# A two-layer decoder trunk on one core: five modulation units from TensorE to wide VectorE units, unit ends spread over later steps, running sums seeded and read by ScalarE

## The chip, the core and the metric

The kernel runs on one NeuronCore of a Trainium2 chip. The metric is the device time of one launch in microseconds (us). Five engines work from their own in-order queues: TensorE (PE; its weight loads are listed apart as PEld), VectorE (DVE), ScalarE (ACT), GpSimd (POOL, hardly used here) and SyncE (SP, which issues nearly all transfers).

## The reference

A trunk of two decoder layers over 256 tokens of width 2048, all in fp32. In both layers a mixer and an MLP are wrapped in RMSNorm and in a modulation by a condition vector `c`:

```python
cond = jax.nn.silu(c)
for i in range(DEPTH):
    mod = cond @ ada_w[i] + ada_b[i]
    sh1, sc1, g1, sh2, sc2, g2 = [m[:, None, :] for m in jnp.split(mod, 6, axis=-1)]
    h = rms_norm(x, norm_mix_g[i]) * (1.0 + sc1) + sh1
    y = even_mixer(h, ...) if i % 2 == 0 else odd_mixer(h, ...)
    x = x + g1 * y
    h = rms_norm(x, norm_mlp_g[i]) * (1.0 + sc2) + sh2
    x = x + g2 * (jnp.square(jax.nn.relu(h @ mlp_up[i])) @ mlp_down[i])
return rms_norm(x, final_norm_g)
```

`ada_w[i]` is 2048 x 12288: each of the six sections (shift, scale, gate; twice) is a product of one vector with a 2048 x 2048 matrix. The even mixer has 16 heads of attention between an input and an output projection, the odd mixer has 8 heads with a forget gate and 8 heads with three branches. `mlp_up` is 2048 x 8192, `mlp_down` 8192 x 2048.

## The kernel before

**Weights.** Every weight comes from HBM once, in pieces of 1 MB, into one of four staging buffers (`wst`); the modulation weights (`wa`) share these buffers with the projections' (`w`). Each fp32 weight is split in two: ScalarE writes the rounded high part `wh` (L306), VectorE the rest `wl` (L308), in halves of 128x1024, two to a piece, with four buffers each. A product is then three TensorE matmuls: high by high, high by low, low by high. A staging buffer is free again when `wl` of its second half is written.

**Passes.** The even input projection and the first half of layer 0's up-projection are streamed by row groups of the contraction: `kproj` (L361) takes one 1 MB piece (one of half that size in the first two groups), 48 matmuls (24), and adds into running sums that lie in SBUF between the groups. Each pass has two sums of 128x512. From the second group on, the second sum is seeded: ScalarE copies it back to PSUM before the matmuls (L370) and out again after them (L390). The first sum starts from zero in PSUM, and VectorE adds it to the stored one afterwards (L392). There are 56 such passes: 4 x 8 in the even projection (`even`, L603), 3 x 8 in the up-projection (`up_streamed`, L659). PSUM holds four `mm` tiles, two passes' worth. Other projections (`proj`, `down`) hold their sums in PSUM through.

**Modulation units.** `ada` (L226) is a generator; one unit computes some columns of one or two sections, in steps of 1 MB. On VectorE a unit accumulates `acc += w * cond[k]` (L245, L248), one operation for each of the 16 k-tiles; on TensorE it makes 16 row products into one `row` bank, four to a step (L241), and ScalarE copies the row to `acc` (L254). The unit's end turns the row into columns: four TensorE transposes for each 512 columns into the single bank `aux` (L258), a reduction on VectorE that empties it (L260), and small operations that write `mod` (L265, L268). The end stands directly behind the last step; a unit of 1024 columns has two such blocks, and the second needs the bank that the first one's reduction empties.

**The order of the work.** `queue` lists the units; `pump` runs one step of the first; `tick` is called after each weight load and pumps by a rate set for each stage; `need(left, keys)` pumps until no more than `left` units of a section are left. So the steps are woven between the loads, and SP issues weights and modulation weights in that order. A scheduler may then move an instruction past its neighbours on its engine, which shows in the order below. The norm of a row group's input (`make_h`) needs its shift and scale, and stands behind a `need`.

**Attention.** `causal_head` (L574) serves 16 even heads and 8 odd ones; VectorE scales both parts of the probabilities (L586, L590).

## Time and profile before

| | |
|---|---|
| Median of 3 runs | 2322.27 us (2320.33 to 2328.7) |
| The profiled execution | 2327.63 us, span of its instructions 2325.8 us |
| TensorE busy | 2243.2 us (96%) |
| TensorE weight loads busy | 2156.4 us (93%) |
| VectorE busy | 1669.5 us (72%) |
| ScalarE busy | 1114.7 us (48%) |
| Moved by the transfers | 599.94 MB, mean 258 GB/s |

The stages in the profile: the even input projection to some 215 us, its last row group with the even attention to some 312 us, the even output projection to some 410 us, the streamed up-projection to some 610 us, the rest of layer 0's MLP to 1180 us, the odd mixer to some 1605 us, and the second MLP to the end. A matmul's end in the profile is modelled and matmuls are pipelined, so a stretch in which TensorE is 96% busy can hold fewer matmuls than it might; the count of records of a stretch and the granted clock tell more. Every fp32 matmul of a row product leaves two records.

### The profile page before, as it was taken

Reading aid. Unit: us, or ns where it says so; the run is one execution under the profiler, and the core shown is the slowest. Engines: PE = TensorE matmul, PEld = TensorE weight load, DVE = VectorE, ACT = ScalarE, POOL = GpSimd, SP = SyncE. Lnnn points to the kernel's source line nnn. Section 1 sums busy time; section 2 is a strip of 40 time slices with the busy share of each in tenths; the row PEclk is TensorE's granted clock in tenths of the full one; section 3 lists DMA queues with packets and bytes.
Section 4 is the critical chain, followed back from the end, with each engine's and each line's share of the span. In section 5 each row is a group of like instructions: output and inputs, shape, how many; then the busy total and the mean of one; then the engine's idle time right before and its main releaser. Section 6 shows DMA issues by size and latency. Waiting matters only on the chain.

```text
span 2325.8 us, 44699 instructions
## 1 busy us (share of the span) xinstructions
PE 2243.2 (96%) x18762; PEld 2156.4 (93%) x18762; DVE 1669.5 (72%) x2456; ACT 1114.7 (48%) x1742; POOL 4.6 (0%) x25
## 2 busy tenths in 40 slices
PE   7899999999999999999999999998999999999998
PEld 5799789899999999999999988998999999999998
DVE  3888888797767777787876988888644654655555
ACT  4555753555744344344444555444544543543543
POOL 0000000000000000000000000000000000000000
PEclk9999999999999999999999999999999999999999
DMA  9899688899978778787857877886655656656652
GB/s 308 322 326 357 228 281 319 278 323 316 321 280 290 271 272 305 274 313 267 311 198 244 310 266 245 329 302 230 197 199 188 194 199 190 192 199 192 191 194 95
DMA packets 285819, 599.94 MB, mean 258 GB/s; under 512 B 14290, under 2 KB 23346, under 8 KB 285618
## 3 DMA queue, kind: packets, MB, share of 16 engines
q1 hardware_dynamic: 285072, 596.34, 74.2%
q8 instruction: 147, 2.41, 0.4%
q10 hardware_dynamic: 546, 0.75, 0.1%
q14 instruction: 54, 0.44, 0.1%
HBM read 594.95 MB, written 2.10 MB: 257 GB/s over the span
## 4 chain that ended last, share of the span: by engine, by line
issue 65%; PE 21%; DVE 7%; DMA 5%; ACT 2%; SPq 0%; POOL 0%; POOLq 0%; DVEq 0%; ACTq 0%
PE mm L386 6%; PE mm L320 6%; DMA wa<-in_ada_w_dram 3%; DVE wl L308 3%; DVE acc L248 2%; PE bank L386 1%; PE row L241 1%; PE mm L329 1%; PE mm L330 1%; PE mm L328 1%; DMA w<-in_odd_w_out_dram 1%; PE bank L593 1%; PE bank L556 1%; ACT wh L306 1%; DVE sacc L155 0%
## 5 line engine op out<-in xcount | busy, mean ns | idle before, releaser
L308 DVE TENSOR_TENSOR wl<-w,wh 128x1024 fp32r<-128x1024 f32 x736 | 878.9, 1220 | 415.2 <-ACT wh L306 414.3
L306 ACT ACTIVATE wh<-w 128x1024 fp32r<-128x1024 f32 x736 | 751.6, 1055 | 855.4 <-PE mm L320 673.4
L320 PE MATMUL mm<-hs,wh 128*128 128x256 f32 x5120 | 886.2, 278 | 3.9 <-DVE hs L408 3.0
L320 PEld LDWEIGHTS mm<-hs,wh 128*128 128x128 f32 x5120 | 776.6, 189 | 5.5 <-DVE hs L408 3.2
L320 PE MATMUL mm<-xs,wh 128*128 128x256 f32 (+1 forms) x4128 | 720.4, 279 | 2.4 <-ACT xs L454 2.2
L320 PE MATMUL mm<-hs,wl 128*128 128x256 f32 x2560 | 711.4, 278 | 4.0 <-DVE wl L308 3.8
L320 PEld LDWEIGHTS mm<-xs,wh 128*128 128x128 f32 (+1 forms) x4128 | 627.8, 189 | 5.6 <-ACT xs L454 3.4
L320 PE MATMUL mm<-xs,wl 128*128 128x256 f32 x2064 | 572.8, 279 | 1.7 <-DVE wl L308 1.6
L320 PEld LDWEIGHTS mm<-hs,wl 128*128 128x128 f32 x2560 | 482.8, 189 | 6.3 <-DVE wl L308 6.0
L248 DVE SCALAR_TENSOR_TENSOR acc<-wa,cond,acc 128x1024 f32<-128x1024 f32 (+1 forms) x360 | 389.1, 1081 | 108.3 <-DMA wa<-in_ada_w_dram 104.0
L320 PEld LDWEIGHTS mm<-xs,wl 128*128 128x128 f32 x2064 | 388.2, 188 | 3.3 <-DVE wl L308 2.8
L386 PE MATMUL mm<-xs,wh 128*128 128x256 f32 x1792 | 318.4, 281 | 0.3 <-ACT wh L306 0.3
L386 PEld LDWEIGHTS mm<-xs,wh 128*128 128x128 f32 x1792 | 273.9, 189 | 19.2 <-issue 9.2
L386 PE MATMUL mm<-xs,wl 128*128 128x256 f32 x896 | 249.6, 279 | 3.1 <-DVE wl L308 3.1
L386 PEld LDWEIGHTS mm<-xs,wl 128*128 128x128 f32 x896 | 169.2, 189 | 4.8 <-DVE wl L308 3.7
L390 ACT ACTIVATE u<-mm 128x512 f32<-128x512 f32 x88 | 51.7, 589 | 70.3 <-PE mm L386 69.5
L565 ACT ACTIVATE p<-p,st 128x128 f32<-128x128 f32 (+1 forms) x96 | 40.2, 420 | 29.3 <-DVE st L579 14.7
L536 ACT ACTIVATE t<-mm 128x256 f32<-128x256 f32 x96 | 36.4, 379 | 34.1 <-PE mm L320 24.6
L386 PE MATMUL mm<-wh,xs 128*128 128x256 f32 x256 | 50.0, 290 | 0.9 <-ACT wh L306 0.8
L258 PE MATMUL aux<-cst,acc 128*128 128x128 f32 x192 | 31.5, 285 | 19.6 <-DVE s L260 10.2
L241 PE MATMUL row<-wa,cond 128*32 128x512 f32 x288 | 47.1, 628 | 2.1 <-DMA wa<-in_ada_w_dram 2.1
L151 ACT ACTIVATE t<-xT 128x256 f32<-128x256 f32 x60 | 24.6, 414 | 45.3 <-DVE xT L471 45.3
(214 smaller groups left out, 1458.2 us busy)
## 6 DMA issues: line engine op xcount, KB each, us to landing
wa<-in_ada_w_dram SPq DMA_DIRECT2D x160, 1024.0 KB, 6.2
w<-in_mlp_up_dram SPq DMA_DIRECT2D x128, 1024.0 KB, 5.7
w<-in_mlp_down_dram SPq DMA_DIRECT2D x128, 1024.0 KB, 5.1
w<-in_odd_w_in_dram SPq DMA_DIRECT2D x44, 1024.0 KB, 5.7
wa<-in_ada_w_dram SPq DMA_DIRECT2D x64, 512.0 KB, 5.9
w<-in_even_w_in_dram SPq DMA_DIRECT2D x27, 1024.0 KB, 7.0
w<-in_even_w_out_dram SPq DMA_DIRECT2D x16, 1024.0 KB, 5.3
w<-in_odd_w_out_dram SPq DMA_DIRECT2D x16, 1024.0 KB, 6.5
```

The costliest lines, as they stand in the source:

```text
L151: A.activation(s, xT[:, kt, :], AF.Square)
L241: T.matmul(row[32 * i:32 * i + 32, :], cond[:, k:k + 1].to_broadcast([128, 32]), w[:, i, :], start=t == 0, stop=t == KT // kn - 1, tile_po ...
L248: V.scalar_tensor_tensor(acc, w[:, i, :], cond[:, k:k + 1], acc, op0=ALU.mult, op1=ALU.add)
L258: T.transpose(ps[:, i, :], acc[:, 512 * b + 128 * i:512 * b + 128 * i + 128], ident)
L306: A.activation(wh, w[:, g:g + KS, :], AF.Copy)
L308: V.tensor_tensor(wl, w[:, g:g + KS, :], wh.bitcast(F32), op=ALU.subtract)
L320: T.matmul(P[0:m, 0:S], st[:, c0:c0 + m], mv, start=f and i == 0, stop=e and i == 2)
L328: T.matmul(Ps[j][:, 0:n], hi, wh[:, c0:c0 + n], start=f, stop=False)
L386: T.matmul(Ps[i][:, 256 * h:256 * h + 256], st, mv, start=first and e == 0, stop=last and e == 2, skip_group_check=True)
L390: A.activation(flat[i], P, AF.Copy)
L536: A.activation(r, P[:, 0:S], AF.Relu)
L565: A.activation(p[:, o:o + n], p[:, o:o + n], AF.Exp, bias=m[:, i:i + 1], accum_out=den[:, i:i + 1])
```

## The change

Five things change.

1. Which units run where. The first gate (section 2) had four TensorE units of 512 columns, and now has two, and one VectorE unit of 1024. The second scale and shift (4 and 3) had eight units of 512 columns, two of them on TensorE, and are now four VectorE units that hold 512 columns of both. The second gate (5) had four units, one on TensorE, and now has two VectorE units of 1024. Five TensorE units go; the number of 1 MB steps stays.
2. The ends. `columns` puts each block of a unit's end on a list; `tick` takes one block from it before it pumps, and `need` empties it.
3. `down` of the even output projection calls `need` for the first gate inside its blocks instead of all of it ahead.
4. `kproj` seeds both sums on ScalarE and reads both out on ScalarE.
5. `NORM_A`: ScalarE scales the 256 wide part of the probabilities.

```diff
-G1_T = "1111"
-SC2_T = "0000"
-SH2_T = "0101"
-G2_T = "0100"
-NORM_A = False
+NORM_A = True
...
                 if t == KT // kn - 1:
...
+                    columns(l, secs, c0, cw, tensor, acc)
                 yield t == KT // kn - 1
+        late = deque()
+
+        def columns(l, secs, c0, cw, tensor, acc):
+            red = s32()
+            blocks = cw * len(secs) // 512
+
+            def block(b):
+                ps = aux((128, 4, 128))
+                for i in range(4):
+                    T.transpose(ps[:, i, :], acc[:, 512 * b + 128 * i:512 * b + 128 * i + 128], ident)
+                src = ps.rearrange("p a (j q) -> p a j q", q=32)[:, :, :, 0] if tensor else ps
+                V.tensor_reduce(red[:, 4 * b:4 * b + 4], src, AX.X, ALU.add)
+                if b < blocks - 1:
+                    return
...
+            for b in range(blocks):
+                late.append(lambda b=b: block(b))
...
         def tick():
+            if late:
+                late.popleft()()
             credit[0] += rate[0]
...
             while sum(k in keys for k, _ in fill) > left:
                 pump()
+            while late:
+                late.popleft()()
...
-            seeded = [g > 0 and not held and i == 1 for i in range(len(outs))]
+            seeded = g > 0 and not held
...
-                        if g == 0 or held or seeded[i]:
-                            A.activation(flat[i], P, AF.Copy)
-                        else:
-                            V.tensor_tensor(flat[i], P, flat[i], op=ALU.add)
+                        A.activation(flat[i], P, AF.Copy)
...
-        def down(W, row0, tiles, order, ev):
+        def down(W, row0, tiles, order, ev, lazy=None):
...
+                    if lazy and n == 3:
+                        need(max(2 - blk, 0), lazy)
...
-                need(3 - g, (l, 3))
+                need(3 - g, (l, 4))
...
+        queue(0, (2,), True, 0, 512)
+        queue(0, (2,), True, 512, 512)
+        queue(0, (2,), False, 1024, 1024)
         for g in range(4):
-            queue(0, (2,), G1_T[g] == "1", 512 * g, 512)
-        for g in range(4):
-            queue(0, (4,), SC2_T[g] == "1", 512 * g, 512)
-            queue(0, (3,), SH2_T[g] == "1", 512 * g, 512)
-        for g in range(4):
-            queue(0, (5,), G2_T[g] == "1", 512 * g, 512)
+            queue(0, (4, 3), False, 512 * g, 512)
+        for c0 in (0, 1024):
+            queue(0, (5,), False, c0, 1024)
...
-        need(0, (0, 2))
-        down(even_w_out[0], 0, o, (2, 3, 0, 1), residual(0, 2, True))
+        down(even_w_out[0], 0, o, (2, 3, 0, 1), residual(0, 2, True), (0, 2))
```

ScalarE in the streamed up-projection, before; the numbers tell buffers apart, `mm` are the passes' sums in PSUM, `u` the stored ones:

```order
L390 ACTIVATE u_4587<-mm_5286 128x512
L370 ACTIVATE mm_5425<-u_4591 128x512
L306 ACTIVATE wh_5479<-w_5477 128x1024
L306 ACTIVATE wh_5483<-w_5477 128x1024
L390 ACTIVATE u_4589<-mm_5356 128x512
L370 ACTIVATE mm_5494<-u_4593 128x512
L306 ACTIVATE wh_5548<-w_5546 128x1024
```

The same place now (L401 is the eviction, L382 the seeding, L318 the split):

```order
L318 ACTIVATE wh_5444<-w_5442 128x1024
L401 ACTIVATE u_4574<-mm_5319 128x512
L382 ACTIVATE mm_5457<-u_4578 128x512
L401 ACTIVATE u_4575<-mm_5320 128x512
L318 ACTIVATE wh_5448<-w_5442 128x1024
L382 ACTIVATE mm_5458<-u_4579 128x512
L318 ACTIVATE wh_5513<-w_5511 128x1024
```

Before, both splits of `w_5477`, whose pass writes `mm_5494`, stood behind the eviction of the pass three before (`mm_5286`). Now the second split of `w_5442`, whose pass writes `mm_5457` and `mm_5458`, stands behind both evictions of the pass two before (`mm_5319`, `mm_5320`).

VectorE in layer 0's MLP, at the end of a layer 1 unit, before; `s` is the reduced end, `aux` the transposes' bank:

```order
L308 TENSOR_TENSOR wl_9516<-w_9509,wh_9515 128x1024
L245 TENSOR_SCALAR acc_9686<-wa_9687,cond_100 128x1024
L260 TENSOR_REDUCE s_9523<-aux_9524 128x4
L308 TENSOR_TENSOR wl_9589<-w_9586,wh_9588 128x1024
L260 TENSOR_REDUCE s_9523<-aux_9530 128x4
L308 TENSOR_TENSOR wl_9593<-w_9586,wh_9592 128x1024
L265 TENSOR_TENSOR mod_99<-s_9523,adab_98 128x8
```

The same unit's end now (L264 is the reduction, L244 the accumulation, L320 the low half):

```order
L320 TENSOR_TENSOR wl_9736<-w_9733,wh_9735 128x1024
L264 TENSOR_REDUCE s_9620<-aux_9679 128x4
L320 TENSOR_TENSOR wl_9740<-w_9733,wh_9739 128x1024
L244 SCALAR_TENSOR_TENSOR acc_9751<-wa_9814,cond_100,acc_9751 128x1024 x2
L320 TENSOR_TENSOR wl_9807<-w_9804,wh_9806 128x1024
L264 TENSOR_REDUCE s_9620<-aux_9743 128x4
L320 TENSOR_TENSOR wl_9811<-w_9804,wh_9810 128x1024
L271 TENSOR_TENSOR mod_99<-s_9620,adab_98 128x8
```

The two reductions stood one low half apart, the first behind the next unit's first operation; they now stand a whole load apart.

TensorE at the third row group of the up-projection, before; the unit whose end `aux_6215` is runs out inside a pass:

```order
L386 MATMUL mm_6223<-xs_96,wl_6199 128x256
L258 MATMUL aux_6215<-cst_94,acc_6213 128x128 x4
L386 MATMUL mm_6223<-xs_96,wh_6198 128x256 x2
L386 MATMUL mm_6223<-xs_96,wl_6199 128x256
L386 MATMUL mm_6222<-xs_96,wh_6198 128x256 x2
L386 MATMUL mm_6222<-xs_96,wl_6199 128x256
```

And now, where `mm_5666` is the last pass of one row group and `mm_5766` the first of the next:

```order
L398 MATMUL mm_5666<-xs_96,wl_5656 128x256
L262 MATMUL aux_5719<-cst_94,acc_5088 128x128 x4
L262 MATMUL aux_5725<-cst_94,acc_5088 128x128 x4
L398 MATMUL mm_5766<-xs_96,wh_5752 128x256
L398 MATMUL mm_5767<-xs_96,wh_5752 128x256
L398 MATMUL mm_5835<-xs_96,wh_5822 128x256
L398 MATMUL mm_5766<-xs_96,wh_5752 128x256
```

The transposes stood inside a pass; at this group and at the next both blocks now stand between two groups' passes.

## Rows read from the trace of the kernel before

**Rows 1.** Five stretches: length, busy us (x records) by engine, granted clock, transfer share, GB/s.

```profile
60.00:215.00 155.00, 139.76 (x1136) 135.84 (x1134) 138.33 (x156) 79.81 (x111) 0.00 (x0) 0.96 0.93 330
215.00:312.00 97.00, 96.54 (x704) 75.19 (x704) 74.29 (x198) 68.81 (x155) 0.00 (x0) 1.00 0.69 248
405.00:640.00 235.00, 225.20 (x1896) 210.56 (x1895) 183.82 (x257) 141.40 (x214) 0.69 (x1) 0.98 0.90 309
640.00:1180.00 540.00, 520.70 (x4473) 515.73 (x4472) 409.58 (x483) 222.84 (x291) 0.00 (x0) 0.98 0.81 287
1605.00:2326.00 721.00, 707.97 (x6186) 704.95 (x6186) 400.08 (x519) 326.25 (x462) 1.31 (x2) 0.99 0.57 183
```

**Rows 2.** TensorE's waits, 640 to 1605 us: who for whom, us in total, times, longest.

```profile
PE aux L258 <- DVE s L260: 9.4, 6, 4.2
PE mm L320 <- DVE wl L308: 5.4, 11, 1.0
...
PE aux L258 <- DVE acc L248: 2.0, 1, 2.0
```

**Rows 3.** TensorE's waits, 405 to 640 us, the longest in total.

```profile
PE aux L258 <- DVE acc L248: 6.1, 3, 3.9
```

**Rows 4.** Timeline of VectorE at 843 us: start, us, operation, [idle before it, ended by].

```profile
843.37 0.75 DVE L245 TENSOR_SCALAR acc<-wa,cond 128x1024 f32<-128x1024 f32 x1 [4.10 <-DMA wa<-in_ada_w_dram]
844.03 0.68 DVE L260 TENSOR_REDUCE s<-aux 128x4 f32<-128x512 f32 x1
844.63 1.21 DVE L308 TENSOR_TENSOR wl<-w,wh 128x1024 fp32r<-128x1024 f32 x1
```

**Rows 5.** Four stretches of 10 us around unit ends, columns as in rows 1.

```profile
495.00:505.00 10.00, 7.79 (x54) 7.79 (x55) 9.67 (x16) 5.94 (x10) 0.00 (x0) 0.83 0.92 322
764.00:774.00 10.00, 8.17 (x58) 7.97 (x57) 6.72 (x10) 2.01 (x2) 0.00 (x0) 0.83 0.61 213
840.00:850.00 10.00, 5.76 (x31) 5.56 (x30) 5.66 (x8) 0.30 (x1) 0.00 (x0) 0.66 0.56 194
...
1588.00:1598.00 10.00, 8.48 (x61) 8.22 (x62) 5.33 (x8) 3.73 (x4) 0.00 (x0) 0.83 0.99 368
```

**Rows 6.** Timeline of TensorE at 528 us, one step of a unit.

```profile
528.07 1.06 PE L241 MATMUL row<-wa,cond 128*32 128x512 f32 x8
529.06 0.50 PE L386 MATMUL mm<-xs,wh 128*128 128x256 f32 x2
```

**Rows 7.** The row products' line, in 215 to 312 and in 405 to 640 us.

```profile
L241 PE MATMUL row<-wa,cond x120: 592/592/617, 220.6 to 311.2; 128*32 128x512 f32 x120
...
L241 PE MATMUL row<-wa,cond x96: 592/616/1062, 407.4 to 610.7; 128*32 128x512 f32 x96
```

**Rows 8.** Groups by line and shape: busy us, mean ns | idle before, ended by.

```profile
L306 ACT ACTIVATE wh<-w 128x1024 fp32r<-128x1024 f32 x736 | 751.6, 1055 | 855.4 <-PE mm L320 673.4 <-PE mm L330 34.2 <-PE mm L386 33.9
L248 DVE SCALAR_TENSOR_TENSOR acc<-wa,cond,acc 128x1024 f32<-128x1024 f32 x225 | 288.1, 1280 | 89.5 <-DMA wa<-in_ada_w_dram 87.3
L248 DVE SCALAR_TENSOR_TENSOR acc<-wa,cond,acc 128x512 f32<-128x512 f32 x135 | 101.0, 748 | 18.8 <-DMA wa<-in_ada_w_dram 16.7
L390 ACT ACTIVATE u<-mm 128x512 f32<-128x512 f32 x88 | 51.7, 589 | 70.3 <-PE mm L386 69.5
L392 DVE TENSOR_TENSOR u<-mm,u 128x512 f32<-128x512 f32 x56 | 38.3, 685 | 8.0 <-PE mm L386 7.9
L370 ACT ACTIVATE mm<-u 128x512 f32<-128x512 f32 x56 | 33.3, 595 | 5.8 <-DVE u L392 5.6
L151 ACT ACTIVATE t<-xT 128x256 f32<-128x256 f32 x60 | 24.6, 414 | 45.3 <-DVE xT L471 45.3
L590 DVE TENSOR_SCALAR p<-p,st 128x256 f32<-128x256 f32 x24 | 8.3, 347 | 0.0
```

**Rows 9.** The chain of waits at 329 us: start, us, what.

```profile
329.44 5.48 PE mm L320 x48
```

**Rows 10.** TensorE's waits, 60 to 215 us, the longest in total.

```profile
PE bank L386 <- ACT xs L454: 6.9, 3, 3.3
```

More of the change, by code (lines that the diff above doesn't have):

```diff
@@ L249, in ada @@
                 if t == KT // kn - 1:
-                    n = cols // 128
-                    red = s32()
                     if tensor:
@@ L254, in ada @@
                         A.activation(acc, row, AF.Copy)
-                    for b in range(n // 4):
-                        ps = aux((128, 4, 128))
-                        for i in range(4):
-                            T.transpose(ps[:, i, :], acc[:, 512 * b + 128 * i:512 * b + 128 * i + 128], ident)
-                        src = ps.rearrange("p a (j q) -> p a j q", q=32)[:, :, :, 0] if tensor else ps
-                        V.tensor_reduce(red[:, 4 * b:4 * b + 4], src, AX.X, ALU.add)
-                    k0, n = c0 // 128, cw // 128
-                    for z, s in enumerate(secs):
-                        m = mod[:, 6 * l + s, k0:k0 + n]
-                        a0 = 96 * l + 16 * s + k0
-                        V.tensor_tensor(m, red[:, n * z:n * z + n], adab[:, a0:a0 + n], op=ALU.add)
-                        if s in (1, 4):
-                            g0 = (0 if s == 1 else 32) + 16 * l + k0
-                            V.scalar_tensor_tensor(m, m, 1.0, colA[:, g0:g0 + n], op0=ALU.add, op1=ALU.mult)
-                yield t == KT // kn - 1
+                    columns(l, secs, c0, cw, tensor, acc)
+                yield t == KT // kn - 1
+        late = deque()
[10 more added lines that the diff above has]
+                    return
+                k0, n = c0 // 128, cw // 128
+                for z, s in enumerate(secs):
+                    m = mod[:, 6 * l + s, k0:k0 + n]
+                    a0 = 96 * l + 16 * s + k0
+                    V.tensor_tensor(m, red[:, n * z:n * z + n], adab[:, a0:a0 + n], op=ALU.add)
+                    if s in (1, 4):
+                        g0 = (0 if s == 1 else 32) + 16 * l + k0
+                        V.scalar_tensor_tensor(m, m, 1.0, colA[:, g0:g0 + n], op0=ALU.add, op1=ALU.mult)
+            for b in range(blocks):
+                late.append(lambda b=b: block(b))
         fill = deque()
@@ L365, in kproj @@
             Ps = held or [mm_tile() for _ in outs]
-            seeded = [g > 0 and not held and i == 1 for i in range(len(outs))]
+            seeded = g > 0 and not held
             flat = [dst.rearrange("p a b -> p (a b)") for _, _, dst in outs]
-            for i, P in enumerate(Ps):
-                if seeded[i]:
+            if seeded:
+                for i, P in enumerate(Ps):
                     A.activation(P, flat[i], AF.Copy)
@@ L382, in kproj @@
                             tri3 = ((hi, wh[:, c:c + n]), (hi, wl[:, c:c + n]), (lo, wh[:, c:c + n]))
-                        first = h == 0 and k == 0 and not seeded[i] and not (held and g)
+                        first = h == 0 and k == 0 and not seeded and not (held and g)
                         last = h == 1 and k == kn - 1 and (end or not held)
```

## Prediction

> **What bounds the kernel now.** I read the summed busy times first, then the stretches, then who waits for whom. TensorE is busy nearly everywhere, but [rows 1] show four regimes. From 1605 us on, TensorE is busy 708 of 721 us and nothing that the change touches can shorten it. In 60 to 215 us VectorE is busy 138 of 155 us and the transfer engines 0.93: three resources are near their limits together. In 215 to 312 us, the even layer's attention, TensorE is busy 96.5 of 97 us, VectorE 74.3 and ScalarE 68.8. In 405 to 640 us, the streamed up-projection, the transfer share is 0.90 and TensorE misses 9.8 us. In 640 to 1180 us it misses 19.3 us, at a mean clock of 0.98.
>
> Much of what TensorE misses is one wait. At the end of a unit four transposes stand in TensorE's queue, and everything behind them waits until VectorE has the unit's sum, or has emptied the one bank that the transposes write. After 640 us these waits are 9.4 and 2.0 us [rows 2], in the up-projection 6.1 us [rows 3]. The worst is seen in [rows 4]: VectorE sits 4.10 us for the transfer of the next unit's weights, the reduction that empties the bank stands behind that, and TensorE's second four transposes behind the reduction. What follows costs again: [rows 5] give the mean granted clock of the 10 us around four such waits as 0.83, 0.83, 0.66 and 0.83. The clock has two levels, 1.2 and 2.4 GHz, so a mean of 0.83 over 10 us loses 1.7 us and 0.66 loses 3.4 us.
>
> **The change part by part.**
>
> *Five units leave TensorE.* A unit is 16 row products in four steps. One step on TensorE runs from 528.07 to 529.06, 0.99 us, and the plain matmuls go on directly behind it [rows 6]. Twenty steps go. Eight records make a step, so the attention stretch holds 120/8 = 15 and the up-projection 96/8 = 12 [rows 7]; all 12 go, and the other 8 go from the first gate's four units, two of which leave TensorE, in the attention. That is 7.9 us in the attention and 11.9 us in the up-projection, 19.8 us in sum, if TensorE sets the pace there (zero if it does not).
>
> *Wide units on VectorE.* 112 operations of 128x1024 at 1.28 us replace 144 of 128x512 at 0.748 us [rows 8]: 143 against 108 us, so VectorE gets 35 us for the five units and the joining of the others. All of it must lie beside TensorE's work.
>
> *Sums by ScalarE.* VectorE loses 56 adds of 0.685 us, 38.4 us, and 24 scalings of 0.347 us, 8.3 us; net of the wide units it has 11 us less. ScalarE gets 56 x (0.595 + 0.589) = 66.3 us, and 24 scalings for which no row stands; the nearest is a plain 128x256 activation of 0.414 us [rows 8], 9.9 us. Less five row copies, each about as long as a seeding, ScalarE gets 73 us on some 1115 of 2326. Cover: 48 matmuls of this shape, one pass, stand in the chain of waits with 5.48 us [rows 9], of which the last one's tail is hidden, so some 5.4 us; ScalarE now needs in that time two splits of 1.055 us, two seedings and two evictions [rows 8], 4.5 us. It fits, with 0.9 us to spare. In the order the second split of a pass now stands behind the evictions of the pass two before, where earlier both stood behind the one three before: the lead falls from about three passes to two. If that cover fails everywhere, the whole 66 us show.
>
> *The attention.* ScalarE there gets 8 x 1.18 us for the last row group's passes and 0.41 us for each of about 12 heads, less two row copies, some 13 us on 68.8, in a stretch that would shrink to 89: 0.92 busy. VectorE loses 9.7 us and gets six or so wide steps of 2.56 us: 0.9 busy. Of the 7.9 us I take half, 4 us; bounds -4 (both engines as tight as the 0.89 of VectorE in 60 to 215 us, where TensorE missed 10%, would eat the gain and more) and 7.9.
>
> *The up-projection.* For: 11.9 us of steps, 6.1 us of waits, 1.7 us of low clock. Against: the order shows that the last step of three units now falls just before a row group's first matmuls, at two of these with both blocks of transposes in front of them. The price of one such place has a row: TensorE waits up to 3.3 us for the first operand of a group in 60 to 215 us [rows 10]. There the blocks are woven into the pass before; here the second reduction, 0.68 us as the one at 844.03 in [rows 4], and its transposes come on top, so 3.3 to 4.5 us; two places at 4 us, and 1.7 us of low clock behind each, cost 11.4 us. Left are 8.3 us. A stretch 8 us shorter needs a transfer share of 0.93, which 60 to 215 us reached, but the second split's later place holds each staging buffer longer; I take 6 us, bounds -6 (all gain lost, both places at 4.5 us with two low stretches) and 14.
>
> *60 to 215 us.* 24 adds, 16.5 us, leave VectorE, which was 0.89 busy, but transfers were at 0.93 and two group ends now come later by up to 1.5 us each because their blocks are no longer woven into the last pass. I take 0, bounds -6 and +6 (a transfer share of 0.97). The Trainium skill (DMA: Bandwidth & Descriptors, Measured) states 425 GB/s for large transfers on a single core. The rows show 330 GB/s at 0.93 of the engines' time, which scales to 355, and the busiest stretch of [rows 5] has 368 at 0.99. By the page's figure transfers would bind neither here nor in the up-projection, and the sum would gain some 8 us more; by the rows it does not.
>
> *Ends spread over later steps, after 640 us.* Each block's transposes now come at the next load, one pass of 5.4 us later, and the two blocks of a unit one pass apart. The longest wait was 4.2 us [rows 2], under one pass, so this cover holds. The 11.4 us of waits and 1.7 + 3.4 + 1.7 = 6.8 us of low clock [rows 5] make 18.2 us. What comes late next is the low half of the next weights: in [rows 4] it is written at 844.63, when TensorE would have had about one pass left from 840. That covers it barely, so I take 16 us; bounds 5 and 18.2.
>
> *The rest.* The need before the output projection now falls inside it, and three forced steps in a row go with it; they are among the 15. The scalings of the odd layer move where TensorE is busy 98%: nothing.
>
> Sum: 4 + 6 + 0 + 16 = 26 us. The profiled execution took 2327.63 us (span 2325.8), 5.4 over the median of 2322.27 us; I take the 26 us from the median: **2296 us**.
>
> **The rivals.**
>
> *More: everything adds.* The attention gives 7.9, the up-projection 14, 60 to 215 us gives 6, the ends 18.2, and the early dips as much again as two of [rows 5], 5: 51 us, 2271 us. For it speaks that VectorE is relieved where it was tightest; against it ScalarE's 0.92 in the attention.
>
> *Only the ends pay.* Transfers pace the first 640 us and the TensorE steps were covered: 16 us, 2306 us. For it speaks the 0.90 to 0.93.
>
> *The waits change places.* VectorE still waits in order for the next unit's transfer, so TensorE waits for the low halves instead of the transposes; there are already 5.4 us of that after 640 us [rows 2]. The ends then give 5 us and the rest 5: 2312 us, no change that can be told.
>
> *ScalarE paces the seeded passes (slower).* Place: the 56 seeded passes up to 610 us. A late transfer holds the first split, behind it stand the evictions, behind them the seedings that TensorE needs for its next pass. The Trainium skill (TensorE: Matmul & The Clock Gate, Part 1) states that ScalarE's queue is strictly first in, first out. That is the rule by which this rival happens; the trace agrees as far as ScalarE stood idle 69.5 us before evictions until TensorE was done [rows 8], with splits queued behind them. Price: 66 us times the share that TensorE sees. It decides from 26/66 = 40% on; at 60% the time is 2322 - 26 + 40 = 2336 us. Against it: 4.5 us of work in a 5.4 us pass.
>
> That the change does not do what it says is excluded by the order: 20 steps, 56 adds and 24 scalings are gone from their engines.
>
> **How the numbers follow.** A measurement of this kernel tells about 0.5%, 11.6 us, from no change. Chances: forecast (2282 to 2309 us) 0.55, more 0.14, only the ends 0.10, waits change places 0.13, ScalarE paces 0.08. Faster by over 0.5% is the first three, 0.79, less 0.02 for the upper tail of "only the ends": 0.77; within 0.5% 0.15; slower 0.08. The range keeps "more" and "waits change places" and leaves out the last rival and half of the tails: 2266 to 2318 us.
>
> **What would show it.** Right: no wait of TensorE at transposes over 1 us after 640 us; mean clock 1.0 where [rows 5] show less; two waits of 3 to 5 us for the operands of the third and fourth group of the up-projection; the attention 3 to 5 us shorter with ScalarE near 0.9. Wrong: TensorE waiting for seedings or splits of ScalarE in most passes before 610 us, or as many microseconds for low halves after 640 us as it now has for transposes.

## The result, and the profile after

The changed kernel takes 2338.66 us (median of 5 runs, 2335.19 to 2342.5), the kernel before in the same comparison 2325.86 us: a ratio of 1.006, 95% interval 1.0041 to 1.008. It is slower by 13 us; 26 us less had been forecast, and the range ended at 2318. The profiled execution's span is 2337.7 us, 11.9 over that of before.

The same stretches as in [rows 1], of the changed kernel (length, busy us and records of TensorE, its weight loads, VectorE, ScalarE and GpSimd, granted clock, transfer share, GB/s):

```profile
60.00:215.00 155.00, 139.50 (x1122) 135.07 (x1124) 123.76 (x124) 104.36 (x158) 0.00 (x0) 0.94 0.93 327
215.00:312.00 97.00, 87.58 (x606) 70.79 (x606) 75.61 (x186) 81.36 (x182) 0.00 (x0) 0.96 0.65 231
...
405.00:640.00 235.00, 206.93 (x1723) 203.87 (x1722) 186.23 (x214) 157.62 (x246) 1.67 (x1) 0.93 0.88 298
640.00:1180.00 540.00, 522.66 (x4530) 516.64 (x4529) 413.57 (x474) 228.60 (x300) 0.00 (x0) 1.00 0.82 291
```

TensorE has less work and does not get done sooner. In 405 to 640 us it was busy 225.2 of 235 us and is now busy 206.9, at a clock of 0.93 instead of 0.98; in the attention 96.5 of 97 us, and now 87.6. In 640 to 1180 us it is busy 2 us more. What it waits for, 405 to 640 us (who for whom, us in total, times, longest), beside [rows 3]:

```profile
PE mm L398 <- ACT xs L463: 10.7, 4, 3.1
PE aux L262 <- DVE s L264: 9.4, 2, 5.2
```

And 640 to 1180 us, beside [rows 2]:

```profile
PE mm L332 <- DVE wl L320: 13.6, 24, 1.7
```

The long waits at transposes after 640 us are gone, as forecast. The waits for low halves (5.4 us in [rows 2]) are 13.6 us.

Cut into three by the weight matmuls in the traces, one profiled execution each: from the start to the first matmul of the streamed up-projection, from there to its last, and from that to the first matmul of the second MLP (us; the ratio is to the kernel before on the same chip). Everything behind that point takes 718 us in both kernels.

| kernel | up to the up-projection | up-projection | on to the second MLP | ratio (95%) |
|---|---|---|---|---|
| before | 417.3 | 199.9 | 990.9 | 1 |
| changed | 423.8 | 204.8 | 991.3 | 1.006 (1.0041 to 1.008) |
| ends_woven | 427.2 | 188.3 | 989.1 | 0.9973 (0.9959 to 0.9986) |
| sums_by_vector | 428.6 | 209.1 | 984.6 | 1.0052 (1.0035 to 1.0069) |
| scaling_by_vector | 419.7 | 206.0 | 985.5 | 1.0029 (1.0014 to 1.0044) |
| only_deferred | 423.1 | 194.1 | 990.9 | 1.001 (0.9995 to 1.0025) |
| only_wide | 426.0 | 190.0 | 989.2 | 0.9994 (0.9972 to 1.0015) |
| woven_scaling_v | 423.8 | 184.3 | 985.0 | 0.993 (0.9903 to 0.9956) |
| woven_inline | 416.4 | 192.1 | 981.4 | 0.9928 (0.9909 to 0.9948) |
| woven_sums_v | 426.0 | 188.0 | 977.9 | 0.9929 (0.9912 to 0.9945) |
| delayed_steps | 422.2 | 185.7 | 987.3 | 0.9945 (0.9923 to 0.9967) |
| deferred_delayed | 422.8 | 195.5 | 992.4 | 1.0026 (1.0006 to 1.0047) |
| steps_behind_low | 424.3 | 184.4 | 959.7 | 0.9812 (0.9791 to 0.9832) |
| deferred_behind_low | 424.6 | 194.6 | 955.0 | 0.9871 (0.9849 to 0.9893) |
| before_behind_low | 420.3 | 198.5 | 963.3 | 0.989 (0.9866 to 0.9914) |
| after_behind_low | 422.8 | 210.9 | 960.3 | 0.9932 (0.9912 to 0.9952) |

The 11.8 us are 6.5 before the up-projection, 4.9 in it and 0.4 behind it. Each third needs its own explanation. How far such a figure can be trusted is seen in the last four kernels: up to the end of the up-projection they have the same program as woven_scaling_v, only_deferred, the kernel before and the changed kernel, and differ from these by 0.5 to 3.0 us ahead of the up-projection and by 0.1 to 6.1 us in it. A difference of a few microseconds between two rows is therefore a hint and no proof; the ratios come from several executions each.

### The profile page after: what moved, and what is told of

Read it like the earlier page. It is cut to its first block, busy times and chain, and to the rows that moved or that the text cites. A ratio compares the mean times of both kernels' runs of the same rounds, so it can differ in the third digit from the quotient of the medians.

```text
span 2337.7 us, 44422 instructions
## 1 busy us (share of the span) xinstructions
PE 2228.4 (95%) x18602; PEld 2155.9 (92%) x18602; DVE 1665.0 (71%) x2341; ACT 1180.1 (50%) x1873; POOL 5.6 (0%) x25
## 4 chain that ended last, share of the span: by engine, by line
PE 38%; issue 34%; DMA 12%; DVE 11%; ACT 4%; SPq 0%; POOL 0%; DVEq 0%; POOLq 0%; ACTq 0%
PE mm L332 22%; DMA wa<-in_ada_w_dram 10%; PE mm L398 8%; DVE wl L320 5%; DVE acc L244 3%; ACT wh L318 1%; PE bank L398 1%; PE mm L342 1%; PE mm L341 1%; PE mm L340 1%; PE bank L604 1%; DMA w<-in_even_w_in_dram 1%; DVE s L264 1%; PE row L237 1%; ACT u L401 1%
## 5 line engine op out<-in xcount | busy, mean ns | idle before, releaser
L320 DVE TENSOR_TENSOR wl<-w,wh 128x1024 fp32r<-128x1024 f32 x736 | 880.2, 1220 | 412.8 <-ACT wh L318 405.7
L318 ACT ACTIVATE wh<-w 128x1024 fp32r<-128x1024 f32 x736 | 752.7, 1055 | 821.9 <-PE mm L332 670.6
L332 PE MATMUL mm<-hs,wl 128*128 128x256 f32 x2560 | 709.7, 277 | 11.4 <-DVE wl L320 11.1
L244 DVE SCALAR_TENSOR_TENSOR acc<-wa,cond,acc 128x1024 f32<-128x1024 f32 x330 | 422.7, 1281 | 140.0 <-DMA wa<-in_ada_w_dram 136.0
L401 ACT ACTIVATE u<-mm 128x512 f32<-128x512 f32 x144 | 83.9, 590 | 58.1 <-PE mm L398 57.2
L382 ACT ACTIVATE mm<-u 128x512 f32<-128x512 f32 x112 | 65.4, 598 | 1.2
```

Source lines behind the costliest of these rows:

```text
L244: V.scalar_tensor_tensor(acc, w[:, i, :], cond[:, k:k + 1], acc, op0=ALU.mult, op1=ALU.add)
L318: A.activation(wh, w[:, g:g + KS, :], AF.Copy)
L320: V.tensor_tensor(wl, w[:, g:g + KS, :], wh.bitcast(F32), op=ALU.subtract)
L332: T.matmul(P[0:m, 0:S], st[:, c0:c0 + m], mv, start=f and i == 0, stop=e and i == 2)
L382: A.activation(P, flat[i], AF.Copy)
L401: A.activation(flat[i], P, AF.Copy)
```

## Experiments on the up-projection

**Where TensorE stands there.** The timeline of the changed kernel at the third row group's start, TensorE, then VectorE, then ScalarE (start, us, operation, [idle before it, ended by]):

```profile
518.86 0.60 PE L262 MATMUL aux<-cst,acc 128*128 128x128 f32 x4
524.63 1.12 PE L262 MATMUL aux<-cst,acc 128*128 128x128 f32 x4 [5.17 <-DVE s L264]
528.87 1.23 PE L398 MATMUL mm<-xs,wh 128*128 128x256 f32 x4 [3.12 <-ACT xs L463]
```

```profile
521.27 1.23 DVE L320 TENSOR_TENSOR wl<-w,wh 128x1024 fp32r<-128x1024 f32 x1 [2.57 <-ACT wh L318]
522.69 1.28 DVE L244 SCALAR_TENSOR_TENSOR acc<-wa,cond,acc 128x1024 f32<-128x1024 f32 x1 [0.20 <-DMA wa<-in_ada_w_dram]
523.89 0.68 DVE L264 TENSOR_REDUCE s<-aux 128x4 f32<-128x512 f32 x1
...
527.79 1.28 DVE L462 SCALAR_TENSOR_TENSOR t<-xT,mod,sacc 128x256 f32<-128x256 f32 x3
```

```profile
520.18 1.06 ACT L318 ACTIVATE wh<-w 128x1024 fp32r<-128x1024 f32 x1 [3.33 <-DMA w<-in_mlp_up_dram]
```

Read from the bottom: a weight transfer lands late, so ScalarE idles 3.33 us and splits at 520.18; VectorE's low half waits for that split, behind it stand a unit step and then the reduction that empties the transposes' bank; TensorE's second four transposes wait 5.17 us for the reduction. Behind them the second reduction and the scale must be done before the group's operands exist: another 3.12 us. The group that starts at 583.25 waits 4.20 and 3.09 us in the same way, the one at 472.90 2.98 us. The stretches around the two worst have a granted clock of 0.68 and 0.66:

```profile
518.00:530.00 12.00, 3.71 (x22) 3.07 (x22) 9.22 (x16) 5.40 (x9) 0.00 (x0) 0.68 0.94 334
573.00:585.00 12.00, 4.71 (x29) 4.07 (x28) 10.97 (x19) 6.31 (x11) 0.00 (x0) 0.66 0.96 337
```

**ends_woven** changes one number of the changed kernel, so that the same units end earlier in the order:

```diff
-R_OUT = 0.7
+R_OUT = 0.9
```

> The changed kernel with one number altered: the rate of modulation steps in the output projection is 0.9 instead of 0.7, so that two more steps are done there and every unit of the up-projection ends one to three passes ahead of its row group instead of at the group's first matmul. Theory A (unit ends that stand at the group boundaries cost the time): the three boundary waits that the trace of the changed kernel shows in the up-projection, 3.7, 8.7 and 7.7 us, fall to 3 us or less each and 3 to 4 us of low clock go with them: 12 to 16 us less than the changed kernel's 2338.7, so 2323 to 2327 us. Theory B (transfers pace the first 640 us and TensorE only waits elsewhere): 2336 to 2339 us, with the waits reappearing as waits for splits. Theory C (ScalarE's seedings pace the passes): 2335 to 2339 us.

Measured: 0.9973 where the changed kernel has 1.006, 0.9 per cent or some 20 us less, at least what theory A asked for. The up-projection takes 188.3 us instead of 204.8. Two steps moved ahead of it with the new number, but that explains little: it moves 60.2 MB there, the changed kernel 61.4. Its stretch and TensorE's longest wait from 405 to 640 us:

```profile
405.00:640.00 235.00, 220.46 (x1886) 217.51 (x1886) 196.91 (x221) 166.22 (x262) 1.60 (x1) 0.98 0.93 322
```

```profile
PE mm L398 <- ACT mm L382: 5.6, 8, 1.7
```

No wait at transposes is left among the longest, the clock is back at 0.98, and the transfers, which theory B took for the limit, move 322 GB/s where they moved 298. A wait for ScalarE's seedings appears, 5.6 us in eight pieces: theory C's mechanism exists, at a twelfth of its full price of 66 us.

**sums_by_vector** and **woven_sums_v** put the running sums back as they were, in the changed kernel and in woven_scaling_v (next section):

```diff
-            seeded = g > 0 and not held
+            seeded = [g > 0 and not held and i == 1 for i in range(len(outs))]
...
-                        A.activation(flat[i], P, AF.Copy)
+                        if g == 0 or held or seeded[i]:
+                            A.activation(flat[i], P, AF.Copy)
+                        else:
+                            V.tensor_tensor(flat[i], P, flat[i], op=ALU.add)
```

> The changed kernel with the running sums as before: of two tiles of a pass only the second is put back into PSUM by ScalarE, the first is added by VectorE. ScalarE does 56 seedings less (33 us of its time), VectorE 56 adds of 0.69 us more (38 us). Theory C (ScalarE paces the seeded passes): 8 us or more less, 2331 us or below. Theory A (group boundaries): the boundaries stand as they were, 2336 to 2341 us; VectorE's chain at a boundary can be up to 2 us longer. Theory D (ScalarE paces the attention stretch, where it is busy 19.8 of 20 us from 255 to 275 us): the eight seedings and evictions of the last row group there go, some 2 to 4 us less, 2335 to 2337 us.

> The kernel of the run woven_scaling_v (ratio 0.993) with the running sums as before, the first of two tiles of a pass added by VectorE: what seeding by ScalarE is worth once the unit ends no longer hide it. If VectorE paces the up-projection (busy 202 of 235 us from 405 to 640 us with the seedings, about 25 us more without), 8 to 15 us slower, ratio 0.997 to 1.000. If not, 0.992 to 0.995, as sums_by_vector was no slower than the changed kernel.

Measured: 1.0052 against 1.006, and 0.9929 against 0.993. Seeding by ScalarE neither paces the passes nor is worth anything that can be told in the whole. In either pair of traces it gives 4 us in the up-projection (209.1 to 204.8, 188.0 to 184.3) and 2 to 5 ahead of it, and stands 7 us behind after it (984.6 to 991.3, 977.9 to 985.0), where the programs of a pair are the same; why is open. Theory C falls, and so do the 8 to 15 us of the second expectation.

## Experiments ahead of the up-projection

**scaling_by_vector** and **woven_scaling_v** set `NORM_A = False` in the changed kernel and in ends_woven.

> The changed kernel with the 24 scalings of attention weights on VectorE (0.35 us each) instead of ScalarE (0.50 us each). Theory D (ScalarE paces the attention, so that the row steps taken off TensorE there gave nothing): 16 scalings lie in the even layer's attention, 8 us of ScalarE's time, of which 3 to 6 us show: 2333 to 2336 us. Theory E (the attention is paced by the order of its heads' chains, or VectorE takes ScalarE's place as it did in the kernel before): 2337 to 2341 us.

> The kernel of the run ends_woven (modulation rate 0.9 in the output projection) with the 24 scalings of attention weights back on VectorE. If the two effects seen apart add (20 us from the woven ends, 7 us from ScalarE's relief in the attention, both against the changed kernel): a ratio of 0.994 to 0.995 to the kernel before, some 2312 to 2315 us where before has 2326. If the scalings' gain only moved the phase of transfers and passes: 0.997, as ends_woven.

Measured: 1.0029 and 0.993, each 0.3 to 0.4 per cent, 7 to 10 us, less than its partner, with intervals that still allow the expected 3 to 6 us; the two effects add. Some 4 us of it lie ahead of the up-projection in either pair of traces (423.8 to 419.7, 427.2 to 423.8). The 20 us in mid-attention, of the kernel before, the changed one and scaling_by_vector:

```profile
255.00:275.00 20.00, 20.00 (x144) 16.62 (x143) 16.62 (x52) 17.23 (x45) 0.00 (x0) 1.00 0.58 209
```

```profile
255.00:275.00 20.00, 19.88 (x147) 16.31 (x145) 16.96 (x48) 19.78 (x50) 0.00 (x0) 1.00 0.65 240
```

```profile
255.00:275.00 20.00, 19.81 (x147) 17.01 (x143) 18.48 (x50) 17.98 (x40) 0.00 (x0) 1.00 0.88 316
```

ScalarE, the fourth busy time, is at 19.78 of 20 us in the changed kernel, as full as TensorE with 19.88; with the scalings back on VectorE it has 17.98.

**only_wide** is the kernel before with the change's first part, the placement of the units, and nothing else:

```diff
-            queue(0, (2,), G1_T[g] == "1", 512 * g, 512)
...
+        queue(0, (2,), True, 0, 512)
+        queue(0, (2,), True, 512, 512)
+        queue(0, (2,), False, 1024, 1024)
+        for g in range(4):
+            queue(0, (4, 3), False, 512 * g, 512)
+        for c0 in (0, 1024):
+            queue(0, (5,), False, c0, 1024)
```

> The kernel before with the placement of units alone: five units leave TensorE (20 row steps of 0.99 us) and become wide VectorE units, their ends whole at one load as before; sums, scalings and the need before the output projection as before. In program order the ends of the up-projection's units stand four, three, two and one passes ahead of the group's end. Theory J (TensorE paces the first 640 us, so the steps count): 10 to 20 us less, 2306 to 2316 us, ratio 0.991 to 0.996. Theory K (transfers and VectorE pace them, so the steps were covered): 2322 to 2330 us, ratio 0.998 to 1.002.

Measured: 0.9994, as theory K said, but not for its reason. The up-projection gives 9.9 us, which is theory J's place; ahead of it 8.7 us are lost. In 215 to 312 us VectorE is busy 83.9 us (74.3 in [rows 1]) and TensorE 88.2:

```profile
215.00:312.00 97.00, 88.24 (x634) 75.36 (x633) 83.88 (x200) 66.60 (x152) 0.00 (x0) 0.96 0.68 237
```

In the up-projection a step that leaves TensorE is worth its time. Where the attention loses is seen when the two traces are set side by side by the number of matmuls done (row products and transposes left out). only_wide is 4.4 us ahead of the kernel before when that kernel is at 295 us, and 8.6 us behind it at 320. So the steps pay in the attention too, and more than that is lost at its end: from 295 to 315 us TensorE is busy 13.3 of 20 us at a clock of 0.82, where the kernel before has 20.0 at 1.00, and the transfers' share is 0.43 instead of 0.63. only_wide keeps the steps that are forced in a row ahead of the output projection, now on VectorE; whether they or VectorE's load as such make the loss, no run tells.

**woven_inline** takes the spreading of the ends out of woven_scaling_v (`block(b)` in place of `late.append(lambda b=b: block(b))`).

> The kernel of the run woven_scaling_v (ratio 0.993) with every unit's end whole at one load, as before, instead of spread over later loads; in the up-projection the ends stand five, four, four and three passes ahead of their groups. If spreading the ends is worth nothing by itself (as only_deferred said of the kernel before): 0.991 to 0.995. If it is worth what the prediction said once the groups are woven: 14 to 18 us slower, ratio 0.999 to 1.001.

Measured: 0.9928 against 0.993. In these traces spreading the ends costs 7.4 us ahead of the up-projection (416.4 against 423.8), gives 7.8 in it (192.1 against 184.3) and nothing behind it (981.4 against 985.0). only_deferred agrees: 5.8 us lost ahead of the up-projection, 5.8 gained in it. The parts don't add ahead of the up-projection: placement 8.7, spreading 6 to 7 and the scalings 4 us make more than the 6.5 of the changed kernel, and woven_inline, which has the placement and ScalarE's sums but neither of the other two, stands at 416.4.

## Experiments behind the up-projection

**only_deferred** is the kernel before with the change's second part alone (`columns`, `late`, and their emptying in `tick` and `need`).

> The kernel before with the spread unit ends alone: each block of transposes is issued at the next load, units, sums and scalings as before. The prediction's term for this after 640 us is 16 us; the changed kernel's trace shows 9 us gained from 640 to 870 us against its own lag and 13.6 us of waits for the low halves, so 8 to 16 us less after 640 us. Up to 640 us the blocks of TensorE units now fall at group ends as well. Theory A: that costs 0 to 6 us there, so 2310 to 2322 us against 2325.9. Theory F (waits change places, low halves instead of transposes): 2323 to 2328 us.

Measured: 1.001, and 990.9 us from the up-projection to the second MLP, to the tenth what it was. TensorE's longest wait from 640 to 1180 us, where [rows 2] have 5.4 us up to 1605:

```profile
PE mm L334 <- DVE wl L322: 17.2, 27, 2.5
```

Theory F: the transposes' waits have become waits for low halves. Why those are late is seen in the changed kernel at 683 us, ScalarE, VectorE and TensorE:

```profile
677.37 1.06 ACT L318 ACTIVATE wh<-w 128x1024 fp32r<-128x1024 f32 x1 [0.18 <-PE mm L332]
...
678.60 1.05 ACT L318 ACTIVATE wh<-w 128x1024 fp32r<-128x1024 f32 x1
```

```profile
675.98 2.35 DVE L320 TENSOR_TENSOR wl<-w,wh 128x1024 fp32r<-128x1024 f32 x2
683.05 1.29 DVE L244 SCALAR_TENSOR_TENSOR acc<-wa,cond,acc 128x1024 f32<-128x1024 f32 x1 [4.72 <-DMA wa<-in_ada_w_dram]
684.26 2.36 DVE L320 TENSOR_TENSOR wl<-w,wh 128x1024 fp32r<-128x1024 f32 x2
```

```profile
685.53 0.38 PE L332 MATMUL mm<-hs,wl 128*128 128x256 f32 x1 [1.74 <-DVE wl L320]
```

The high halves are written by 679.7, so their low halves could be computed from then on. VectorE stands 4.72 us for the next unit step's transfer and takes them up only at 684.26; TensorE waits. It is the same picture as in [rows 4], which shows 4.10 us, the reduction and then the low half: take the reduction away and the low half is the next in line.

The order of VectorE's queue says the same. In the trace of the kernel before 85 of 156 steps are done, to their last operation, ahead of both low halves of a load whose transfer was issued before theirs, in the changed kernel 105 of 176. Here is VectorE's order in woven_scaling_v in the odd layer, where the transfers are issued as w_14720, wa_14730, w_14782, wa_14792:

```
L244 SCALAR_TENSOR_TENSOR acc_13052<-wa_14730,cond_100,acc_13052 128x1024 x2
L320 TENSOR_TENSOR wl_14723<-w_14720,wh_14722 128x1024
L320 TENSOR_TENSOR wl_14727<-w_14720,wh_14726 128x1024
L244 SCALAR_TENSOR_TENSOR acc_13052<-wa_14792,cond_100,acc_13052 128x1024 x2
...
L320 TENSOR_TENSOR wl_14785<-w_14782,wh_14784 128x1024
```

Each step stands ahead of the low halves of the load that was transferred just before it.

**delayed_steps** and **deferred_delayed** tried to move the steps back by computing each at the `tick` behind the one that issues its transfer, in woven_scaling_v and in only_deferred:

```diff
+                due.append(step)
...
         def tick():
+            while due:
+                due.popleft()()
             if late:
```

> The kernel of the run woven_scaling_v with every unit step computed one load later than its transfer is issued, so that VectorE does the low halves of the load in between before it stands for the step's transfer. Theory G (after 640 us TensorE waits for low halves because VectorE, in order, stands for the next step's transfer, 8.2 us in 640 to 1180 us of ends_woven): these waits fall to under 3 us, and the time is 5 to 10 us less than woven_scaling_v. Theory H (the staging buffers are what is short: a step's buffer is held one load longer, so the next transfers are issued later): no gain or 5 us and more slower, with TensorE waiting for splits that wait for transfers.

> The kernel of the run only_deferred (the kernel before with spread ends alone) with every unit step computed one load later than its transfer is issued. There the waits of TensorE for transposes were gone and those for low halves had risen from 5.4 to 17.2 us in 640 to 1180 us. Theory G (VectorE stands for the step's transfer, low halves behind it): these fall to under 5 us and the time is 8 to 14 us below only_deferred (ratio to the kernel before 0.995 to 0.998). Theory H (a buffer held longer delays the transfers): ratio 1.00 or above, the waits for low halves remain or become waits for the high halves.

Measured: 0.9945 and 1.0026, no gain, as theory H said. But the order shows that these runs tell nothing of theory G: the scheduler put the steps where they had been. Counted in the same way, 81 of 156 still stand ahead of earlier low halves in deferred_delayed (84 in only_deferred), 80 of 176 in delayed_steps (81 in woven_scaling_v); only 7 and 9 moved behind a later load. With the next edit 2 of 156 are left in deferred_behind_low. VectorE's wait for the steps' transfers from 640 to 1180 us, in only_deferred and then in deferred_delayed, is the same too:

```profile
DVE acc L248 <- DMA wa<-in_ada_w_dram: 91.3, 34, 6.3
```

```profile
DVE acc L250 <- DMA wa<-in_ada_w_dram: 92.7, 40, 6.1
```

**steps_behind_low**, **deferred_behind_low**, **before_behind_low** and **after_behind_low** put the order in the program: from the first hidden MLP on, each step is queued behind the last low half that was issued before it. The same edit in woven_scaling_v, in only_deferred, in the kernel before and in the changed kernel:

```diff
-                    hold = after("V")
+                    hold = tc.issue_after(low[0]) if behind[0] else after("V")
...
-                    V.tensor_tensor(wl, w[:, g:g + KS, :], wh.bitcast(F32), op=ALU.subtract)
+                    low[0] = V.tensor_tensor(wl, w[:, g:g + KS, :], wh.bitcast(F32), op=ALU.subtract).ins
...
         rate[0] = R_M0
+        behind[0] = True
```

> The kernel of the run woven_scaling_v with VectorE's queue altered from the first hidden MLP on: every unit step is queued behind the low halves of the loads that were issued before it. In the order of woven_scaling_v two thirds of the steps there stand ahead of one to four low halves of earlier loads, and so did most in the run delayed_steps, whose edit moved only a few of them. Theory G (TensorE waits for low halves because VectorE, in order, stands for a step's transfer ahead of them: 10.4 us from 640 to 1180 us): these waits fall under 4 us and the time by 5 to 12 us, ratio to the kernel before 0.988 to 0.991. Theory H (transfers or staging buffers pace the stretch from 617 to 1608 us, which took 991 us in the kernel before, in the changed kernel and in only_deferred): no change within 3 us, or slower, since the steps release their buffers later.

> The kernel of the run only_deferred with the same alteration of VectorE's queue from the first hidden MLP on (its own time from 617 to 1608 us was 991 us, as in the kernel before, with 17.2 us of waits for low halves in place of 5.4 and of 8.7 for transposes). Theory G: the waits for low halves fall under 6 us and the time by 8 to 14 us, ratio 0.995 to 0.998 where only_deferred had 1.001. Theory H: ratio 1.000 to 1.005.

Measured: 0.9812 where woven_scaling_v has 0.993, and 0.9871 where only_deferred has 1.001: 27 and 32 us less, more than twice what theory G asked for, and theory H is out. Among VectorE's longest waits there is none for a step's transfer any more; its longest from 640 to 1180 us in steps_behind_low is for ScalarE's high halves, and TensorE has no wait for low halves there:

```profile
DVE wl L321 <- ACT wh L319: 89.0, 63, 3.1
```

TensorE's longest there, 617 to 1180 us, where the changed kernel has 16.1 us for low halves:

```profile
PE mm L333 <- ACT xs L464: 2.6, 2, 1.5
```

and the stretch in steps_behind_low, deferred_behind_low, before_behind_low and after_behind_low, one after the other:

```profile
640.00:1180.00 540.00, 534.69 (x4669) 532.71 (x4668) 435.53 (x521) 240.16 (x322) 1.28 (x13) 0.99 0.84 294
```

```profile
640.00:1180.00 540.00, 535.94 (x4686) 534.29 (x4685) 439.51 (x532) 240.58 (x322) 1.26 (x13) 0.99 0.84 294
```

```profile
640.00:1180.00 540.00, 533.90 (x4657) 530.71 (x4657) 437.62 (x530) 238.27 (x317) 1.26 (x13) 0.99 0.84 293
```

```profile
640.00:1180.00 540.00, 536.21 (x4694) 535.28 (x4693) 435.27 (x511) 242.66 (x324) 1.28 (x13) 0.99 0.85 301
```

> The kernel before with VectorE's queue altered alone: from the first hidden MLP on every unit step is queued behind the low halves of the loads issued before it; unit ends whole, units, sums and scalings as before. If TensorE's waits in the hidden MLP were all the order of VectorE's queue: as deferred_behind_low, 0.985 to 0.989. If spread ends are worth the prediction's term once that order is mended (the four transposes of an end, whole at one load, wait for VectorE's last step, now later): 8 to 16 us slower than deferred_behind_low, 0.990 to 0.995.

> The changed kernel with VectorE's queue altered in the same way and nothing else: its three group boundaries in the up-projection and its attention stand as they are. If the order of VectorE's queue was what took back the spread ends' gain after 640 us: the stretch from the up-projection's end to the second MLP, 991 us in the changed kernel, falls to 955 to 965 us, ratio to the kernel before 0.991 to 0.995 (the changed kernel: 1.006). If the stretch is bound otherwise: 1.000 to 1.006.

Measured: 0.989 for the order alone, with the ends whole, and 0.9932 for the changed kernel. The order by itself gives 27.6 of the 35.9 us that the stretch loses with spread ends too (963.3 and 955.0 against 990.9). Between 0.989 and 0.9871 the intervals overlap, so whether spread ends are worth a few microseconds once the order is mended stays open; more than the difference of 8 us in that stretch they are not. The changed kernel's stretch falls to 960.3 us, as expected; its up-projection, 210.9 us, still has the two worst group ends:

```profile
PE aux L263 <- DVE s L265: 13.6, 2, 6.9
```

steps_behind_low beats both kernels: 2286.48 us (median of 4) beside 2331.49 for the kernel before on that chip.

## Why the prediction was wrong

By its own terms: attention and what is ahead of it -4 us forecast, +6.5 measured; up-projection -6, +4.9; behind it -16, +0.4; in sum -26, +11.8.

**Ends after 640 us: the cover was assumed to hold.** The step that failed is "That covers it barely, so I take 16 us". The prediction saw that the low half is late next, gave TensorE one pass in reserve, and kept 16 of 18.2 us. It also misread its row: 844.63 in [rows 4] is where the low half starts. It is written 1.21 us later, at 845.84, which is 5.84 us after 840, and a pass lasts 5.4; by its own rows the cover fails. only_deferred shows that nothing was left: 17.2 us of waits for low halves, and the same 990.9 us. In the changed kernel the prediction's own sign of being wrong is there: 13.6 us for low halves where transposes had cost 11.4. The rival "the waits change places" had the mechanism, and got 0.13. What the prediction did not draw from [rows 4] is the cause common to both waits, VectorE standing for a transfer with ready work behind it; the behind_low runs show that this cause, not the transposes, held some 28 us of the stretch. The forecast that came true is the clock's: with 24 waits of at most 1.7 us, 640 to 1180 us stand at 1.00, where [rows 1] have 0.98. Counted at the same matmuls the changed kernel did gain some 10 us between 670 and 1162 us of the kernel before; in the 60 us ahead of that, at the start of the stretch, it had lost 8.

**Up-projection: two places at 4 us were three at 3.4, 8.3 and 7.3 us.** The mechanism was named; the size was wrong. The price was built from [rows 10] plus a free-standing reduction of 0.68 us. In the trace the reduction stands behind a low half and a step, and these behind late transfers, so the waits for it, 5.17 and 4.20 us, come on top. The first group's place, with one block at the boundary, was left out. The three places make 19.0 us where 8 were taken, 11 us more, and the term missed by 10.9; that the two agree so closely is luck, since the same program took 210.9 us there in after_behind_low and 204.8 here. The low clock was not mis-sized: in the two stretches of 12 us at 0.68 and 0.66 TensorE ran only 3.71 and 4.71 us, and half speed can cost at most half of that, some 4 us, where 3.4 were taken. (For the same reason the prediction counts the clock too high where TensorE waits: in the row of [rows 5] with 0.66 it ran 5.76 of 10 us, so 2.9 us are the most, and 3.4 were taken.) The "for" side was sound: with the ends woven the stretch is 11.6 us shorter than before (ends_woven), near the 11.9 us of row steps.

**Attention and what is ahead of it: the gain came and was lost again.** Half of the steps' time was taken as gain, with a bound of 4 us lost if both vector engines are tight. Counted at the same matmuls the changed kernel is 5.9 us behind the kernel before at 215 us, level with it at 295 us (0.5 ahead), and 5.7 behind at 320. So the attention did give the steps' time, nearly to its end. The term of 0 for 60 to 215 us came out near its bound of 6; it leaves out that the spread ends cost 6 to 7 us ahead of the up-projection (only_deferred, woven_inline). And what the attention had gained went in its last heads, before and now:

```profile
295.00:315.00 20.00, 20.00 (x155) 15.66 (x155) 13.76 (x35) 11.23 (x24) 0.00 (x0) 1.00 0.63 211
```

```profile
295.00:315.00 20.00, 15.28 (x74) 11.98 (x72) 17.60 (x37) 14.18 (x28) 0.00 (x0) 0.74 0.44 149
```

The prediction had no term for this place. SyncE waits 12.6 us there for a low half of VectorE's before it can issue the output projection's next transfer, and only_wide shows the same loss; what starts it stays open. ScalarE came out at 19.78 of 20 us in mid-attention and 0.84 over the whole stretch, where 0.92 was forecast.

**The slower rival was the wrong one.** Slower was given 0.08, all of it to ScalarE's seedings. sums_by_vector rules them out as the cause. The change came out slower by misses with one sign: 60 to 215 us and the up-projection near the bad end of their ranges, the attention at about nothing, and the ends, the largest term, at nothing where at least 5 us had been kept.

The transfers did not bind as the sum supposed. woven_scaling_v moves 333 GB/s from 405 to 640 us at a share of 0.95, against 298 in the changed kernel. That fits a rate which follows TensorE's waits, since buffers come free later while it waits; it was not tested by itself.

## What to carry to other kernels

Where an in-order engine waits for a transfer, look at everything that stands ready behind the waiting instruction, and who waits for the last of it; removing the first victim of such a wait only uncovers the second. Look for it in the engine's order beside the order of the transfers, and state the order in the program, because an edit that only moves code can leave the scheduler's order as it was. Spread work must still end ahead of the point that needs it: unit ends that fell at three groups' first matmuls cost some 20 us here, and one rate constant took them away.

## What had not been expected of the hardware

VectorE's 98 to 112 us of waits for the steps' transfers from 640 to 1180 us (the kernel before to deferred_delayed) did not come from a lack of transfer rate: with the steps queued later they are gone, at 294 GB/s where [rows 1] have 287. And TensorE's stretch of 991 us got 28 to 36 us shorter when they went, although the waits that [rows 2] name there are 17 us. In the trace of deferred_behind_low, 36 us shorter, 22 us are TensorE's idle time (32.4 us of 991.0 before, 10.8 of 955.0). The other 14 are in its busy time, 958.6 and 944.2 us for the same matmuls (7948 and 7952 records), where no list of waits shows them. The granted clock, 0.99 and then 1.00 over the stretch, is a part of it; the rest is open.
